# The output projection as a seven-product block form, product by product, with the up blocks laid out from it

## The chip, the cores and the metric

The kernel runs on one core of a Trainium2 chip. The metric is the time of one execution on the device in microseconds. Three runs of the kernel before took 1751.15, 1747.36 and 1748.91 us; the median is 1748.91 us. The core has five engines with queues of their own, which are worked off in order: TensorE (PE, matrix products into the accumulators in PSUM), VectorE (DVE), ScalarE (ACT), GpSimd (POOL) and SyncE (SP), which here issues the transfers between HBM and the on-chip memory. They wait for each other through semaphores.

## The reference

One layer of a hybrid decoder on 1032 tokens (1024 of a prompt, 8 single steps), width 1024:

```
proj = rmsnorm(x) @ w_in                  # split among two head groups
o_a  = HGRN2(q, k, v, f)                  # 8 heads of 128: 1024 columns
y    = SSD(xs, B, C, dt)                  # 16 heads of 64: 1024 columns
x    = x + concat([o_a, y]) @ w_out       # w_out: 2048 x 1024   <- the stage that changes
h    = rmsnorm(x, norm2_w)
gate, val = split(h @ w_up, 2)            # 2 x 2816 columns
x    = x + (silu(conv3(gate)) * val) @ w_down
y    = rmsnorm(x)
```

All data are 32-bit floats. Everything in the kernel is transposed: 128 features on the partitions, tokens along the free dimension.

## The kernel before

**Precision.** A product of 32-bit floats is made as three products of rounded parts: a weight tile is split into wh (rounded by ScalarE) and wl (the rest, by VectorE), rows into a high and a low part in the same way, and TensorE adds wh x high, wh x low and wl x high (`steps`, L305; all matmuls are recorded at L94).

**Stages.** The input projection runs as 52 jobs of 72 matmuls with 344 tokens each. The eight HGRN heads follow one another; the matmuls of a head are interleaved with the input projection of a later one (`drive`). Each head leaves its 128 rows in HBM (mix_d, eight head rows and eight state-space rows of 128 x 1032; L1055). Then comes the output projection, then the up projection, 22 jobs of 168 matmuls, then the down projection. Up and down already use a form with seven block products in place of eight (2 x 2 blocks of features in, features out and tokens): for the up projection it needs, for each instance of 516 tokens, seven blocks of rows p1 to p7, some of them sums and differences of normalised rows, each as a high and a low part. Down takes sums of weight blocks; these are made ahead, under the heads, by `down_sums`: load half a MB into the buffer wq (L193), four additions on GpSimd (L1202), store to wsum_d (L1204), load the next into the same buffer. There are 22 such items.

**The output projection before.** Jobs a, b, c, d: a is the state-space rows of the first 516 tokens, b the head rows of these tokens, c and d the same of the second 516. Each job multiplies 8 row tiles with one of 8 column tiles for two strips of 258 tokens, 48 matmuls; together 16 row tiles x 8 column tiles x 4 strips x 3 = 1536 matmuls of 258 tokens. The rows come back from mix_d (tile mx), are split on ScalarE (L1109) and VectorE (L1110); weights come as ws and are split at L1093 and L1094. ScalarE copies a's and c's result out of PSUM, VectorE adds b's and d's to it (L1168). The residual x is loaded token-major (xs, xd), turned by transposes on TensorE (four of 128 tokens and one small remainder for each of 16 items, L852 and L854) and added by VectorE (L847). Of each finished strip ScalarE squares the values, GpSimd sums the squares (n2r), and `set_norm` makes from them the inverse root on TensorE, ScalarE and VectorE (L698 to L701). `set_of(i)` then lays out instance i's seven blocks: normalisation on VectorE (L1320), the high part on ScalarE, the low part on VectorE (L1331, L1352), block sums on VectorE or GpSimd (L1336, L1348). Instance 0 is complete after job b, so that its blocks are laid out under c and d; instance 1's follow at the end of d and under the first up job.

**What sets the order.** TensorE's order is written out by hand: a step is one matmul, `after(n, ...)` and `spread(pieces, n)` place the other engines' work n steps later or every n steps. The scheduler orders the other engines from there. All transfers go through SP's queue in program order. A transfer into a buffer waits there until the buffer is free, and so does whatever stands behind it.

## Time and profile before

| what | value |
|---|---|
| median of three runs | 1748.91 us |
| the profiled execution | 1748.51 us, span 1746.6 us |
| busy: TensorE, VectorE, ScalarE, GpSimd | 98%, 68%, 48%, 28% of the span |
| first matmul of the output projection | at 831.25 us |
| first up job | begins at 1054.3 us |
| transfers | 239 MB, mean 137 GB/s |

The span runs from the first to the last recorded instruction; some 1.9 us of the execution lie around it. The page gives busy times over the whole span; a table by stretches, as quoted later, has in each row the stretch, its length, then for TensorE (PE), its weight loads (PEld), VectorE, ScalarE and GpSimd the busy time and number of instructions, then the granted clock (1.00 is full), the share of the DMA engines' time, and GB/s. A row of a group has its line, engine, operation, output and inputs, shapes, count, then busy time in us and the mean in ns, then idle time ahead of it and what ended it. A row of the timeline or the chain has the start, the duration and the count.

### The profile page before, as it was taken

The page shows a single profiled execution, that of the slowest core. Times are in us where ns is not written, and L with a number is a line of the kernel's source. Part 1 is how long each engine was busy: PE and PEld are TensorE (multiplying, and loading weights), DVE is VectorE, ACT ScalarE, POOL GpSimd, SP SyncE. Part 2 cuts the span into 40 slices and gives each one's busy share as a digit, 9 for nine tenths or more (in the row PEclk, how much of TensorE's full clock was granted, in tenths as well). Part 3 has the DMA queues.
Part 4 walks back from the last instruction along what each step waited for, and adds up shares of the span by engine and source line. Part 5 has one row for each costly group of instructions (what it writes and reads, how often), then busy time and mean ns, then how long its engine had stood idle before and what let it go on. Part 6 is the DMA issues. An engine that isn't in the chain of part 4 may idle for free.

```text
span 1746.6 us, 39082 instructions
## 1 busy us (share of the span) xinstructions
PE 1704.6 (98%) x15967; PEld 1650.3 (94%) x15967; DVE 1180.5 (68%) x2053; ACT 838.3 (48%) x1507; POOL 485.6 (28%) x500
## 2 busy tenths in 40 slices
PE   7999999999999999999999998999999999999998
PEld 7999998998999999999899998999999999999998
DVE  4657888467755655664755678867777777775664
ACT  6478688443443444444344444334433334444344
POOL 1102242111433422440102124554445554000001
PEclk9999999999999999999999999999999999999999
DMA  5133574563444443444556442323333323786463
GB/s 158 37 82 93 144 211 139 154 178 120 147 140 127 133 147 111 139 131 124 159 169 204 127 136 58 104 92 95 101 113 113 92 92 96 251 270 229 152 190 123
DMA packets 319689, 239.31 MB, mean 137 GB/s; under 512 B 18380, under 2 KB 287734, under 8 KB 319494
## 3 DMA queue, kind: packets, MB, share of 16 engines
q1 hardware_dynamic: 319222, 236.72, 45.1%
q8 instruction: 125, 2.05, 0.5%
q14 instruction: 54, 0.44, 0.1%
q0 software_dynamic: 288, 0.10, 0.0%
HBM read 178.18 MB, written 58.77 MB: 136 GB/s over the span
## 4 chain that ended last, share of the span: by engine, by line
PE 41%; DVE 4%; DMA 2%; ACT 1%; issue 1%; SPq 1%; DVEq 0%; ACTq 0%
PE ub L94 13%; PE dn L94 11%; PE ua L94 9%; PE mm L94 7%; DMA at<-act_d 1%; DMA ws<-in_w_out_dram 1%; DVE x L1320 1%; DVE wl L1094 0%; PE fin L1761 0%; SPq L193 0%; DVE ul L1331 0%; DMA x<-x_d 0%; DVE wl L1441 0%; DMA act_d<-fext 0%; DVE fcv L370 0%
## 5 line engine op out<-in xcount | busy, mean ns | idle before, releaser
L94 PE MATMUL mm<-hh,wh 128*128 128x344 f32 x1248 | 406.5, 326 | 0.0
L94 PE MATMUL mm<-hl,wh 128*128 128x344 f32 x1248 | 403.9, 324 | 0.0
L94 PE MATMUL mm<-hh,wl 128*128 128x344 f32 x1248 | 402.9, 323 | 0.0
L94 PEld LDWEIGHTS mm<-hh,wh 128*128 128x128 f32 x1248 | 234.9, 188 | 2.9 <-issue 0.9
L94 PEld LDWEIGHTS mm<-hh,wl 128*128 128x128 f32 x1248 | 235.1, 188 | 2.1 <-issue 1.0
L94 PEld LDWEIGHTS mm<-hl,wh 128*128 128x128 f32 x1248 | 234.9, 188 | 2.2 <-issue 0.9
L94 PE MATMUL ub<-uh,wh 128*128 128x258 f32 x704 | 199.4, 283 | 2.1 <-DVE fext L1491 1.6
L94 PE MATMUL ub<-ul,wh 128*128 128x258 f32 x704 | 199.6, 283 | 1.5 <-DVE ul L1352 1.5
L94 PE MATMUL ub<-uh,wl 128*128 128x258 f32 x704 | 198.8, 282 | 0.0
L94 PE MATMUL mm<-mx,wh 128*128 128x258 f32 x1024 | 190.9, 286 | 3.2 <-DVE mx L1110 2.3
L94 PEld LDWEIGHTS mm<-mx,wh 128*128 128x128 f32 x1024 | 158.5, 189 | 5.2 <-DVE mx L1110 2.7
L94 PE MATMUL dn<-at,wh 128*128 128x260 f32 (+1 forms) x896 | 163.1, 282 | 0.0
L94 PE MATMUL ua<-uh,wh 128*128 128x258 f32 x528 | 149.2, 283 | 1.1 <-ACT us L1463 0.6
L94 PE MATMUL ua<-ul,wh 128*128 128x258 f32 x528 | 148.9, 282 | 0.0
L94 PE MATMUL ua<-uh,wl 128*128 128x258 f32 x528 | 148.4, 281 | 0.0
L94 PE MATMUL mm<-mx,wl 128*128 128x258 f32 x512 | 145.4, 284 | 1.7 <-DVE wl L1094 1.7
L94 PEld LDWEIGHTS dn<-at,wh 128*128 128x128 f32 x896 | 137.6, 188 | 0.0
L1202 POOL TENSOR_TENSOR wq<-wq 128x256 f32<-128x256 f32 x88 | 83.3, 947 | 189.0 <-DMA wq<-in_w_down_dram 149.6
L94 PEld LDWEIGHTS ub<-uh,wh 128*128 128x128 f32 x704 | 132.9, 189 | 2.5 <-ACT uh L1330 1.8
L94 PEld LDWEIGHTS ub<-ul,wh 128*128 128x128 f32 x704 | 133.1, 189 | 1.9 <-DVE ul L1352 1.9
L94 PEld LDWEIGHTS ub<-uh,wl 128*128 128x128 f32 x704 | 133.1, 189 | 0.0
L94 PE MATMUL dn<-at,wl 128*128 128x260 f32 (+1 forms) x448 | 126.6, 283 | 2.8 <-DVE wl L1607 2.8
(341 smaller groups left out, 3711.9 us busy)
## 6 DMA issues: line engine op xcount, KB each, us to landing
ws<-in_w_in_dram SPq DMA_DIRECT2D x52, 512.0 KB
ws<-in_w_up_dram SPq DMA_DIRECT2D x44, 512.0 KB
at<-act_d SPq DMA_DIRECT2D x77, 258.0 KB
ws<-in_w_out_dram SPq DMA_DIRECT2D x36, 512.0 KB
wq<-in_w_down_dram SPq DMA_DIRECT2D x44, 256.0 KB
wsum_d<-wq SPq DMA_DIRECT2D x22, 512.0 KB
mx<-mix_d SPq DMA_DIRECT2D x32, 258.0 KB
csb<-cs_d SPq DMA_DIRECT2D x32, 256.0 KB
```

Of the source, the lines that this page charges most:

```text
L94: PE.matmul(out, lhsT, rhs, start=start, stop=stop)
L1202: G.tensor_tensor(out, x_, y_, op=ALU.add)
L1320: V.scalar_tensor_tensor(x_, x_, col("n2", m), rs, op0=ALU.mult, op1=ALU.mult)
```

## The change

The output projection becomes seven products as well. The 2048 rows are one block of state-space rows and one of head rows, the columns two halves (h = 0, 1), and the tokens are, for each instance i, the first and second 258 (c = 0, 1). The products run one after another, each over both instances: p1 (state-space rows, c = 0), p7 (state-space rows c = 0 less c = 1), p4, p6, p5, p2 (head rows, c = 0), p3. Each has 4 column tiles x 2 instances x 24 matmuls, so 7 x 192 = 1344 in all. p3 is cut into p3a (instance 0) and p3b (instance 1).

- The sums of weight blocks for p4 to p7 come from 16 new items ahead of the 22 for down, now 20 steps between an item's parts instead of 26 (`weight_sums`).
- The rows for p5, p6 and p3 are sums and differences of a head's rows and a state-space tile. Each head makes them when it is done (`row_sums`): it loads the state-space tile into its tile k, GpSimd makes three sums 516 wide, SP stores three half rows in row_d. The differences for p7 are made on VectorE when they are loaded.
- Results are combined out of PSUM as `out_add` says; the columns of c = 1 are complete after p5, those of c = 0 with h = 0 after p2, with h = 1 after p3.
- The residual is taken in 16 items of two feature tiles and 258 tokens, with four transposes and two small ones each, under p6, p5 and p2.
- The normalisation multiplies by the feature's weight on ScalarE and by the token's inverse root on VectorE. The blocks that need only c = 1 (p4, p5) are laid out under p2 and p3a (`second_halves`), the other five by `first_halves`, for instance 0 under p3b and for instance 1 in the first up job. This job takes p5 and p4 of both instances first, then the other five of instance 0, then those of instance 1.

```diff
+        fetch(k[:, :NT], mix_d[8 + h])
...
+        spread(row_sums(h, k, sg), 14)
+    def halves(t):
+        return t.rearrange("p (i c t) -> p i c t", i=2, c=2)
+    ROWS = ("p5", "p6", "p3")
+    MID = 2 * QW
+    row_d = dram.tile([3, 8, P, MID], F32, name="row_d")
+    def row_sums(h, k, sg):
+        a, b = halves(k[:, :NT]), halves(sg[:, :NT])
+        yield
+        yield
+        G.tensor_tensor(b[:, :, 1], a[:, :, 1], b[:, :, 1], op=ALU.subtract)
+        G.tensor_tensor(a[:, :, 0], b[:, :, 1], a[:, :, 0], op=ALU.subtract)
+        G.tensor_tensor(b[:, :, 0], a[:, :, 0], b[:, :, 0], op=ALU.add)
+        yield
+        for n, t in enumerate((b[:, :, 1], a[:, :, 0], b[:, :, 0])):
+            SP.dma_start(row_d[n, h].rearrange("p (i t) -> p i t", i=2), t)
...
+    def row_load(p, rs):
+        for r in rs:
+            hi, lo = (t.bitcast(F32).rearrange("p (i t) -> p i t", i=2) for t in (rows[p][r][:, :MID], rows[p][r][:, MID:]))
+            if p in ROWS:
+                fetch(lo, row_d[ROWS.index(p), r].rearrange("p (i t) -> p i t", i=2))
+            else:
+                fetch(lo, halves(mix_d[r if p in ("p2", "p4") else 8 + r])[:, :, 1 if p == "p4" else 0])
+            if p == "p7":
+                fetch(hi, halves(mix_d[8 + r])[:, :, 1])
...
+            if p == "p7":
+                d = tl("e", "dif")[:, :MID]
+                vbehind(lambda: V.tensor_tensor(d, x_, hi.bitcast(F32), op=ALU.subtract))
+                x_ = d
...
+    def out_add(p, i, m, ps):
+        x_ = lambda h, c: xf(i, h, c)[:, m]
+        if p == "p1":
+            mark[0] = A.copy(x_(0, 0), ps)
+        elif p == "p7":
+            mark[0] = A.copy(x_(1, 1), ps)
+        elif p == "p4":
+            vmark[0] = V.tensor_tensor(x_(0, 1), x_(1, 1), ps, op=ALU.add)
+        elif p == "p6":
+            vmark[0] = V.tensor_tensor(x_(1, 0), x_(0, 0), ps, op=ALU.add)
+            G.tensor_tensor(x_(0, 1), x_(0, 1), x_(1, 0), op=ALU.add)
+        elif p == "p5":
+            vmark[0] = V.tensor_tensor(x_(1, 0), ps, x_(1, 0), op=ALU.subtract)
+            G.tensor_tensor(x_(1, 1), x_(1, 0), x_(1, 1), op=ALU.subtract)
+            final(i, 0, 1, m)
+            final(i, 1, 1, m)
+        else:
+            h = int(p == "p3")
+            vmark[0] = V.tensor_tensor(x_(h, 0), x_(h, 0), ps, op=ALU.add)
+            final(i, h, 0, m)
...
+    def weight_sums():
+        yield from pair_sums(w_out[0].rearrange("(two i p) (gv h c) -> h i p two gv c", two=2, p=P, gv=2, h=2), wo_d, 1, 8)
+        yield from pair_sums(w_down[0].rearrange("(i two p) (gv h c) -> h i p two gv c", two=2, p=P, gv=2, h=2), wsum_d, 0, DK)
...
-    job("conv", None, once(lambda: (spread(conv_states(), 60), spread(down_sums(), 26))))
+    job("conv", None, once(lambda: (spread(conv_states(), 60), spread(weight_sums(), 20))))
...
-    for m in range(KT):
-        out_job(f"a{m}", 8, 0, m, begin={0: open_a, 2: ahead_b}.get(m))
-    for m in range(KT):
-        out_job(f"b{m}", 0, 0, m, begin={0: open_b}.get(m))
-    for m in range(KT):
-        out_job(f"c{m}", 8, 1, m, begin={0: open_c}.get(m), depth=3 if m < 7 else 4)
-    for m in range(KT):
-        out_job(f"d0{m}", 0, 1, m, (0,), {0: lambda: split_rest(0, 1)}.get(m), m > 3, "ttwwttww"[m], 2, 4)
-    for m in reversed(range(KT)):
-        out_job(f"d1{m}", 0, 1, m, (1,), pool="wwwwttww"[m], lead=2 if m > 1 else 1, depth=(2, 3, 3, 4, 4, 4, 5, 6)[m])
...
+    for p in OUT[:6]:
+        for m in range(4):
+            out_job(f"{p}_{m}", p, m, begin=begins.get((p, m)), depth=4 if (p, m) == ("p2", 3) else 3)
+    for m in range(4):
+        out_job(f"p3a{m}", "p3", m, (0,), {0: lambda: split_rest("p3")}.get(m), True, "ttww"[m], 2, 4)
+    for m in range(4):
+        out_job(f"p3b{m}", "p3", m, (1,), depth=4 - m if m else 4)
...
+    def normed(i, h, c):
+        x_ = xf(i, h, c)
+        r = rst(i, c).unsqueeze(1).to_broadcast([P, 2, QW])
+        for q in TWO:
+            for m in range(q.start, q.stop):
+                behind(lambda: A.activation(x_[:, m], x_[:, m], AF.Copy, scale=col("n2", 4 * h + m)))
+            vbehind(lambda: V.tensor_tensor(x_[:, q], x_[:, q], r, op=ALU.mult))
             yield
-        c0, c1 = slice(0, QW), slice(QW, MID)
-        if i == 0:
-            yield from norm(0)
-            yield from norm(1)
-            yield from put("p2", a2, "big")
-            yield from put("p4", b2, "e")
-        else:
-            yield from norm(1, c0)
-            yield from put("p2", a2, "big")
-            yield from norm(0, c0)
-            yield from put("p1", a1, "hT")
-            yield from norm(1, c1)
-            yield from put("p4", b2, "hT")
-            yield from norm(0, c1)
-        sa, sb = (quads(tl(tag, "sm")[:, :NT]) for tag in ("xe", "xc"))
-        if i:
-            yield from comb(sb, G, a1, b1, ALU.subtract)
-            yield from comb_put("p5", "hT", sa, b1, b2, ALU.subtract)
-            yield from comb_put("p6", "hT", sa, two(sa), a1, ALU.subtract)
-            yield from put("p7", [sb], "big")
-            yield from comb_put("p3", "big", sa, two(sa), a2, ALU.add)
-            return
-        yield from comb(sa, V, b1, b2, ALU.subtract)
-        yield from comb(sb, G, a1, b1, ALU.subtract)
-        while "c7" not in done:
+    def comb(t, x_, y_, op):
+        for q in TWO:
+            vbehind(lambda: V.tensor_tensor(t[:, q], x_[:, q], y_[:, q], op=op))
             yield
-        yield from put("p1", a1, "hT")
-        yield from put("p5", [sa], "hT")
-        yield from comb(sa, V, two(sa), a1, ALU.subtract)
-        yield from put("p6", [sa], "hT")
-        yield from put("p7", [sb], "hT")
-        yield from comb(sa, V, two(sa), a2, ALU.add)
-        yield from put("p3", [sa], "big")
+    def put(i, name, src, *tags):
+        hi, lo = (tl(tag, "u", F32R) for tag in tags)
+        hq, lq = quads(hi[:, :NT]), quads(lo[:, :NT])
+        usets[i][name] = hq, lq
+        for q in TWO:
+            setmark[0] = A.copy(hq[:, q], src[:, q])
+            vbehind(lambda: V.tensor_tensor(lq[:, q], src[:, q], hq[:, q].bitcast(F32), op=ALU.subtract))
+            yield
...
+    def second_halves(i):
+        b1, b2 = xf(i, 0, 1), xf(i, 1, 1)
+        yield from normed(i, 0, 1)
+        yield from normed(i, 1, 1)
+        sas[i] = quads(tl("xe", "sm")[:, :NT])
+        yield from comb(sas[i], b1, b2, ALU.subtract)
+        yield from put(i, "p4", b2, "big", "e" if i else "big")
+        while i and "p2_3" not in done:
+            yield
+        yield from put(i, "p5", sas[i], *(("hT", "hT") if i else ("e", "big")))
+    def first_halves(i):
+        a1, a2, b1, sa = xf(i, 0, 0), xf(i, 1, 0), xf(i, 0, 1), sas[i]
+        yield from normed(i, 0, 0)
+        yield from put(i, "p1", a1, "hT", "hT")
+        yield from comb(sa, sa, a1, ALU.subtract)
+        yield from comb(b1, a1, b1, ALU.subtract)
+        yield from put(i, "p6", sa, "hT", "hT")
+        yield from put(i, "p7", b1, "hT", "big")
+        yield from normed(i, 1, 0)
+        yield from comb(sa, sa, a2, ALU.add)
+        yield from put(i, "p2", a2, "hT", "big")
+        yield from put(i, "p3", sa, "hT", "big")
...
-    FIRST = ("p1", "p2", "p4", "p5", "p6", "p7", "p3")
+    FIRST = ("p5", "p4", "p1", "p6", "p7", "p2", "p3")
...
-        after(36, lambda: spread(set_of(0), 14))
...
+        after(20, lambda: set_norm(0, 1))
+        after(34, lambda: set_norm(1, 1))
+        sets = chain(second_halves(0), second_halves(1))
+        after(40, lambda: spread(sets, 9))
+        finish("p2_3")
...
+        finish("p3a3")
+        after(28, lambda: set_norm(0, 0))
+        sets0 = first_halves(0)
+        after(32, lambda: spread(sets0, 3))
+        for m in range(3):
+            finish(f"p3b{m}")
+            after(3, lambda m=m: up_split(0, m))
+        finish("p3b3")
+        for _ in chain(sets, sets0):
...
-        after(24, lambda: spread(second, 1))
-        for _ in ups(0, [(name, i) for i in range(2) for name in FIRST]):
+        after(24, lambda: spread(first_halves(1), 3))
+        for _ in ups(0, [(name, i) for names in (FIRST[:2], FIRST[2:]) for i in range(2) for name in names]):
```

What moves on VectorE, where the output projection runs into the up projection. Before, these rows stand ahead of the eviction of product p6 for the first instance in the first up job (us, the last row; x1 are the output columns, n2r the inverse root, uh and ul the parts of a block, sm a block sum):

```order
L701 SCALAR_TENSOR_TENSOR n2r_125_798<-nt_1502_12513,n2r_125_798 128x258
L1320 SCALAR_TENSOR_TENSOR x1_1375_11574<-x1_1375_11574,vcol_99,n2r_125_798 128x258 x2
L1320 SCALAR_TENSOR_TENSOR x1_1394_11727<-x1_1394_11727,vcol_99,n2r_125_798 128x258 x2
L1331 TENSOR_TENSOR ul_1507_12539<-x1_1375_11574,uh_1506_12538 128x516
L1320 SCALAR_TENSOR_TENSOR x1_1327_11246<-x1_1327_11246,vcol_99,n2r_125_798 128x258
L1331 TENSOR_TENSOR ul_1507_12539<-x1_1394_11727,uh_1506_12538 128x516
L1320 SCALAR_TENSOR_TENSOR x1_1327_11246<-x1_1327_11246,vcol_99,n2r_125_798 128x258
L1320 SCALAR_TENSOR_TENSOR x1_1350_11406<-x1_1350_11406,vcol_99,n2r_125_798 128x258 x2
L1348 TENSOR_TENSOR sm_1508_12554<-x1_1327_11246,x1_1375_11574 128x516
L1348 TENSOR_TENSOR sm_1508_12554<-x1_1350_11406,x1_1394_11727 128x516
L1467 TENSOR_TENSOR us_1523_12618<-us_1499_12498,ub_1522_12605 128x258
```

Now these are the last rows ahead of the same eviction (u are the parts of a block); 28 more rows of the same kinds stand ahead of them, behind the addition of p3b's first product:

```order
L1370 TENSOR_TENSOR x1_1134_9737<-x1_1134_9737,n2r_1357_11510 128x516 x2
L1375 TENSOR_TENSOR sm_1459_12208<-sm_1459_12208,x1_1134_9737 128x516
L1384 TENSOR_TENSOR u_1523_12656<-x1_1134_9737,u_1522_12655 128x516 x2
L1375 TENSOR_TENSOR sm_1459_12208<-sm_1459_12208,x1_1134_9737 128x516
L1375 TENSOR_TENSOR x1_1262_10862<-x1_1134_9737,x1_1262_10862 128x516 x2
L1384 TENSOR_TENSOR u_1529_12691<-sm_1459_12208,u_1528_12690 128x516 x2
L1384 TENSOR_TENSOR u_1532_12704<-x1_1262_10862,u_1531_12703 128x516 x2
L1370 TENSOR_TENSOR x1_1305_11176<-x1_1305_11176,n2r_1357_11510 128x516 x2
L1375 TENSOR_TENSOR sm_1459_12208<-sm_1459_12208,x1_1305_11176 128x516 x2
L1384 TENSOR_TENSOR u_1536_12739<-x1_1305_11176,u_1535_12738 128x516
L1489 TENSOR_TENSOR us_1537_12742<-us_1533_12718,ub_1534_12720 128x258
```

All that is left of both instances' blocks but for three low parts now stands in front of this eviction; before, instance 0's blocks were long done there and most of instance 1's sums and low parts stood behind it.

What moves on SP's queue, between the last head and the third product. Before, the rows of the next part and its weights follow each other (ws are weights, mx rows, x1_d the stores of finished columns):

```order
L193 DMA mx_1257_10672<-mix_d_123 128x516
L193 DMA mx_1258_10674<-mix_d_123 128x516
L1179 DMA x1_d_797<-x1_1139_9673 128x258
L1081 DMA ws_1263_10738<-in_w_out_dram 128x8x128
L1179 DMA x1_d_797<-x1_1139_9673 128x258
L1401 DMA ws_1370_11564<-in_w_up_dram 128x8x128
L1401 DMA ws_1371_11566<-in_w_up_dram 128x8x128
L1179 DMA x1_d_797<-x1_1139_9673 128x258
L1081 DMA ws_1270_10804<-in_w_out_dram 128x8x128
```

Now, at the corresponding place, loads and stores of the weight sums (wq, wsum_d) stand between the row loads and the next product's weights:

```order
L193 DMA mx_1248_10783<-row_d_797 128x516
L193 DMA wq_1243_10705<-in_w_down_dram 128x2x256 x2
L193 DMA mx_1249_10784<-row_d_797 128x516
L193 DMA mx_1250_10785<-row_d_797 128x516
L193 DMA mx_1251_10786<-row_d_797 128x516
L193 DMA mx_1252_10787<-row_d_797 128x516
L1264 DMA wsum_d_800<-wq_1243_10705 128x8x128
L193 DMA mx_1253_10788<-row_d_797 128x516
L193 DMA mx_1254_10789<-row_d_797 128x516
L193 DMA mx_1255_10790<-row_d_797 128x516
L193 DMA wq_1259_10819<-in_w_down_dram 128x2x256 x2
L1125 DMA ws_1263_10864<-wo_d_799 128x1024
```

Each of these items still waits for its buffer and for GpSimd, and the weight ws that closes the piece, of p4's last column tile, now stands behind two of them.

At the end of a head (here the last), its store of rows (mix_d) is now followed by the row sums:

```order
L1075 DMA mix_d_123<-sg_1104_9566 128x1032
L193 DMA wq_1235_10611<-in_w_down_dram 128x2x256 x2
L1125 DMA ws_1241_10698<-wo_d_799 128x1024
L193 DMA mx_1207_10402<-mix_d_123 128x2x258
L1094 DMA row_d_797<-sg_1104_9566 256x1x258
L1094 DMA row_d_797<-k_1068_9169 256x1x258
L1094 DMA row_d_797<-sg_1104_9566 256x1x258
L1264 DMA wsum_d_800<-wq_1235_10611 128x8x128
```

The three stores to row_d and the load of the state-space tile are new in each head; before, the head's store was the last of it.

360 lines of the change are left out of this document (162 added, 198 removed).

## The prediction

> **What bounds the kernel now.** I read the page first (busy shares, the slices, the costliest groups), then the same busy times by stretches of the output projection, then the chain of waits inside it.
>
> ```profile
> span 1746.6 us, 39082 instructions
> PE 1704.6 (98%) x15967; PEld 1650.3 (94%) x15967; DVE 1180.5 (68%) x2053; ACT 838.3 (48%) x1507; POOL 485.6 (28%) x500
> L94 PE MATMUL mm<-mx,wh 128*128 128x258 f32 x1024 | 190.9, 286 | 3.2 <-DVE mx L1110 2.3
> L94 PE MATMUL mm<-mx,wl 128*128 128x258 f32 x512 | 145.4, 284 | 1.7 <-DVE wl L1094 1.7
> ```
>
> TensorE is busy for 98% of the span, so removed matmuls come off the end, unless another engine then holds TensorE up. The output projection is the two mm<-mx groups: 1024 + 512 = 1536 matmuls. Their mean of 286 ns is not their price, because they overlap; the chain gives the price:
>
> ```profile
> 957.59 5.96 PE mm L94 x48
> 963.55 0.44 PE xtp L852 x4
> 963.98 0.15 PE xtd L854
> 964.14 5.98 PE mm L94 x48
> ```
>
> 48 matmuls take 5.97 us, 0.1244 us each. The four residual transposes of an item take 0.44 us (0.11 each) and the small one 0.15.
>
> ```profile
> core 0: us, PE busy (x) PEld busy (x) DVE busy (x) ACT busy (x) POOL busy (x), PEclk, DMA share, GB/s
> 900.00:950.00 50.00, 50.00 (x417) 49.81 (x416) 23.43 (x36) 18.75 (x33) 9.06 (x13) 1.00 0.67 200
> 1000.00:1020.00 20.00, 18.77 (x153) 18.16 (x151) 15.49 (x20) 11.17 (x16) 4.05 (x3) 1.00 0.49 132
> 1020.00:1040.00 20.00, 19.76 (x161) 19.50 (x162) 12.63 (x23) 8.75 (x16) 6.84 (x6) 1.00 0.42 119
> 1040.00:1060.00 20.00, 18.86 (x153) 18.34 (x152) 14.96 (x24) 9.53 (x17) 8.24 (x9) 1.00 0.50 146
> 1060.00:1080.00 20.00, 16.38 (x131) 15.61 (x130) 19.96 (x32) 8.88 (x17) 8.08 (x8) 1.00 0.00 1
> 1080.00:1100.00 20.00, 19.37 (x162) 19.16 (x161) 17.43 (x28) 9.56 (x17) 11.17 (x9) 1.00 0.27 81
> ```
>
> In the middle of the output projection (900 to 950) TensorE never stops and VectorE is half idle. Where it runs into the up projection (1000 to 1100), TensorE is idle for 1.23 + 0.24 + 1.14 + 3.62 + 0.63 = 6.9 us, and from 1060 to 1080 VectorE is busy for 19.96 of 20 us: there, for a moment, VectorE is the bound, laying out the second set of up blocks.
>
> **The matmuls.** Seven products of 192 matmuls make 1344, against 1536. 192 x 0.1244 = **-23.9 us**; the pace of the up projection, which I expect as the other bound, is a little faster per matmul, 5.79 / 48 = 0.1206:
>
> ```profile
> 1083.27 5.79 PE ub L94 x48
> ```
>
> That would make it 23.2 us. The residual is still 16 items, each now with four transposes and two small ones: one more of 0.15 each, **+2.4 us** on TensorE's own queue, which nothing hides.
>
> **The layout of the up blocks.** This is the large term. Before, the first token half is finished in the middle of the stage and its seven blocks are laid out while TensorE runs on and VectorE is half idle. Now both instances finish last, and the blocks that need the last product's columns are all laid out between that product and the first up job. VectorE works in order, so I count its rows. From the addition after p3b's first product to the eviction of p6 for the first instance (us_1537; the second instance's p6 needs its accumulator) stand 8 normalisations, 12 block sums and 19 low-part differences 516 wide, 7 weight differences 512 wide, 5 additions 258 wide and two inverse roots of three operations. Rows that price them:
>
> ```profile
> L1094 DVE TENSOR_TENSOR wl<-ws,wh 128x1024 fp32r<-128x1024 f32 x35 | 45.1, 1288 | 18.2 <-ACT wh L1093 17.5
> L1168 DVE TENSOR_TENSOR x<-x,mm 128x258 f32<-128x258 f32 x32 | 13.4, 418 | 13.1 <-PE mm L94 13.1
> L1331 DVE TENSOR_TENSOR ul<-x,uh 128x516 fp32r<-128x516 f32 x12 | 8.2, 712 | 1.9 <-ACT uh L1330 1.8
> L1441 DVE TENSOR_TENSOR wl<-wt,wh 128x512 fp32r<-128x512 f32 x8 | 5.7, 738 | 0.2 <-ACT wh L1440 0.2
> ...
> 1058.06 0.42 DVE L699 SCALAR_TENSOR_TENSOR nt<-n2ms,n2r 128x258 f32<-128x258 f32 x1
> 1058.51 0.85 DVE L700 SCALAR_TENSOR_TENSOR nt<-nt,n2r 128x258 f32<-128x258 f32 x1
> 1059.40 1.39 DVE L701 SCALAR_TENSOR_TENSOR n2r<-nt,n2r 128x258 f32<-128x258 f32 x1
> ...
> 1067.01 2.21 DVE L1348 TENSOR_TENSOR sm<-x,x 128x516 f32<-128x516 f32 x2
> 1069.14 0.41 DVE L1467 TENSOR_TENSOR us<-us,ub 128x258 f32<-128x258 f32 x1
> 1069.48 1.29 DVE L1352 TENSOR_TENSOR ul<-sm,uh 128x516 fp32r<-128x516 f32 x2
> 1070.69 1.29 DVE L1348 TENSOR_TENSOR sm<-sm,x 128x516 f32<-128x516 f32 x2
> 1071.90 0.41 DVE L1475 TENSOR_TENSOR us<-us,ua 128x258 f32<-128x258 f32 x1
> ```
>
> In an unbroken run two 516-wide operations take 1.21 us from start to start (1069.48, 1070.69, 1071.90), so 0.605 each: the floor. The group means (0.71, 0.74) are the ceiling, and the pair at 1067.01, with an operation of GpSimd beside it, took 2.21. Floor: 46 x 0.605 + 5 x 0.34 (1069.14 to 1069.48) + 2 x 2.77 (1058.06 to 1060.83) = 27.8 + 1.7 + 5.5 = 35.0 us. Ceiling: 39 x 0.71 + 7 x 0.74 + 5 x 0.42 + 5.5 = 40.5. Count from the end of p3a: the first of these rows can start when the first p3b product is done, 24 x 0.1244 = 3 us on, and I add 1 us for two places where VectorE waits for ScalarE's root. So the eviction is done 39 to 44.5 us after p3a. Behind it TensorE still has the second instance's p6, p7, p2 and p3 of that up job, 48 matmuls or 5.8 us, with two evictions between, some 7 us: the job ends 46 to 51.5 us after p3a. Without a wait it would be 96 matmuls of p3b and the job's 168: 11.9 + 20.3 = 32.2 us. TensorE loses 14 to 19 us. I take the lower half, **+16 us**, since most rows are the streaming kind. The 6.9 us of today's wait at the same place are inside this count, so they come off: **-6.9 us**.
>
> One stage earlier, under p2 and p3a, 58 VectorE instructions (wl, the halves for the second columns, the row differences, the residual) sum at the floor to 6 x 1.29 + 26 x 0.605 + 13 x 0.34 + 4 x (0.605 + 0.15) + 5.5 = 36 us, against 11 groups of 24 matmuls and four residual items on TensorE: 264 x 0.1244 + 4 x 0.74 = 35.8. That is 0 to 4 us over, and the three accumulators let TensorE lead by as much: I take **+1 us**, keeping 5 as its upper end. Under p6 and p5 it is about 20 us of VectorE for 24 us of TensorE: nothing.
>
> **The queue that issues transfers.** SP issues in order. Rows of the trace for the weight sums that already exist:
>
> ```profile
> 589.04 1.04 POOL L905 TENSOR_TENSOR vb<-vb,k 128x512 f32<-128x512 f32 x1 [6.70 <-DMA vb<-vd_d]
> 594.55 5.17 POOL L1202 TENSOR_TENSOR wq<-wq 128x256 f32<-128x256 f32 x4
> 607.40 3.50 POOL L1202 TENSOR_TENSOR wq<-wq 128x256 f32<-128x256 f32 x4 [7.69 <-DMA wq<-in_w_down_dram]
> ...
> 582.37 0.34 SPq L1055 DMA_DIRECT2D mix_d<-sg  x1
> ...
> 599.74 0.37 SPq L1204 DMA_DIRECT2D wsum_d<-wq  x1
> 603.15 1.20 SPq L193 DMA_DIRECT2D wq<-in_w_down_dram  x2
> 610.92 0.36 SPq L1204 DMA_DIRECT2D wsum_d<-wq  x1
> 613.06 0.38 SPq L200 DMA_DIRECT2D ws<-in_w_in_dram  x1
> 614.13 1.21 SPq L193 DMA_DIRECT2D wq<-in_w_down_dram  x2
> ...
> 644.45 0.34 SPq L1055 DMA_DIRECT2D mix_d<-sg  x1
> ...
> 626.21 1.05 ACT L203 CAST wh<-ws 128x1024 fp32r<-128x1024 f32 x1 [2.59 <-PE mm L94]
> ```
>
> One item (load, four GpSimd sums, store, all in one buffer) takes 614.13 - 603.15 = 11 us: landing 4.25, sums 3.5, store and return 3.2. There are now 38 items instead of 22, 60 steps of the order apart instead of 78. Per head of 288 steps that is 4.8 items: 52.8 us, about 7 more where the head's own GpSimd work stands ahead (589.04 to 594.55, and a slower sum of 5.17), about 4 for the three new row sums, that is 64 us in a head of 62 (from 582.37 to 644.45, when the rows of one head and of the next leave). The lag of about 2 us per head piles up to 10 to 13 over six and a half heads. A weight that is issued at 613.06 is cast at 626.21; with 4.25 us of landing, 8.9 us of lag cost nothing before the cast, and more is hidden behind it, as the next job's weights are cast while the last ones are in use. I take **0**, 0 to 8 from the rows, and the other end is a rival.
>
> From head 7's end to p6 the queue carries, one behind another, seven weights, four sum loads and three stores of half a MB, the head's rows, three row stores and nine row loads: 11.0 MB, and p4's last weight stands behind two sum items of 11 to 12 us each. By the issue times this weight is 0 to 10 us late; **+3 us**, nearer the low end as the weight before it is already there.
>
> ```profile
> GB/s 158 37 82 93 144 211 139 154 178 120 147 140 127 133 147 111 139 131 124 159 169 204 127 136 58 104 92 95 101 113 113 92 92 96 251 270 229 152 190 123
> ```
>
> The volume alone, 11.0 MB in the 36 us that TensorE needs until then (288 matmuls at 0.1244), asks for 306 GB/s, where the best slice has 270; at 270 it takes 41 us, 5 us more, which one job's lead (48 matmuls, 6 us) just hides. The Trainium skill (DMA: Bandwidth & Descriptors, Specifications) puts the limit of HBM per core at about 358 GB/s; by that the 11.0 MB fit in 31 us and this bound falls away. No slice of the row above comes near it, so the row keeps its place as the upper side.
>
> The clock is a second place. The column PEclk stands at 1.00 in every stretch above, but none of them holds a long wait. The Trainium skill (TensorE: Matmul & The Clock Gate, HAM oscillation) says that an idle gap over about 3.4 us sends TensorE back to half clock for a while; if the new wait comes as two or three such gaps, its figure of 1.67 us at half pace makes an estimate of about 2 us more on top of the sum. The rows above neither show nor exclude it.
>
> **The sum.** -23.9 + 2.4 + 16 - 6.9 + 1 + 0 + 3 = **-8.4 us**. Against the profiled execution's 1748.5 us (span 1746.6 and 1.9 around it; the median of the three runs, 1748.9, is 0.4 above) that is **1740 us**. Its own bounds: 14 for the layout and 0 for the queue give 1734, 19 with 1 + 4 and 6 give 1750.
>
> **The rivals.**
> *A, the saving arrives whole*: the layout hides as well as today, -23.9 + 2.4 = 1727 us. For it: VectorE has 32% of the span idle. Against it: that idle time lies in other stages, and in the place that counts VectorE is already full from 1060 to 1080 with fewer operations.
> *B, the layout eats it all*: the ceiling prices, with GpSimd's sums beside them as at 1067.01, make the wait 19 us plus 4 under p2, the queue 6: 1749 us, no change.
> *C, slower*: the chain of weight sums. If an item takes 11.6 us rather than 11 (the sums took 3.5 in one row and 5.17 in the other), a head needs 4.8 x 11.6 + 11 = 66.7 us against 62.1; from the point where the lag passes the 8.9 us of cover, TensorE goes at the queue's pace: 4.6 x 6.5 - 8.9 = 21 us, 1761 us. For it: one buffer, in order, and the new row stores behind the same queue. Against it: in the trace SP often waits beside these items without TensorE noticing.
> *D, the change doesn't shorten what it should*: the matmuls fall but take longer each (their rows are now two strips of 258); then the sum lacks its 23.9 us, 1764. Against it: each matmul still reads one strip of 258.
>
> **Chances.** The forecast 0.43, A 0.14, B 0.12, C 0.28, D 0.03. A difference under 0.2% (3.5 us) is what a measurement of this kernel can't tell from none. The forecast's own range, 1734 to 1750, lies mostly beyond that: 0.38 faster, 0.04 within, 0.01 slower. With A that is 0.52 faster; B gives 0.09 within and 0.03 on the faster side; C and D 0.31 slower. So faster 0.55, the same 0.13, slower 0.32. The range reaches from just under A to D, a little over C's price: 1726 to 1764.
>
> **What will show it.** Right: 1344 mm matmuls at 0.124 us each; TensorE whole from p7 to p5 but for about 3 us in p4; at the change to the up projection one stretch of 40 us or so in which VectorE is full and TensorE loses 14 to 19 us, waiting for the evictions us and the blocks ul. Wrong: TensorE waits for new weights during the heads, and these for SP's turn (C); waits of less than 8 us at the transition (A); or waits inside p4 and p6 for weights above 10 us. The forecast falls if the heads no longer take about 62 us each, as I have given that nothing.

## The result, and the profile after

The changed kernel takes 1873.03 us (median of six runs, 1863.98 to 1875.5) against 1749.65 us for the kernel before (six runs): 1.0698 of its time, 95% interval 1.0675 to 1.0722. The forecast was 1740 us, with a range up to 1764. One execution of the kernel before, beside the last runs, took 2051.3 us at a granted clock of 0.753 and is left out of all comparisons. The page of the changed kernel:

```profile
span 1873.7 us, 39110 instructions
PE 1725.9 (92%) x15791; PEld 1664.7 (89%) x15791; DVE 1222.5 (65%) x2086; ACT 849.6 (45%) x1544; POOL 595.2 (32%) x600
L94 PE MATMUL mm<-mx,wh 128*128 128x258 f32 x896 | 179.1, 298 | 14.2 <-ACT wh L1136 7.7
```

896 and 448 matmuls (the second group is not shown) are the 1344 that were expected. TensorE is idle for 147.8 us of the span, before for 42.0. And it is busy for 21.3 us longer, although 21.5 us of work by the forecast's prices were taken out: the mean matmul of this group takes 298 ns, not 286. Where the stages begin is seen from the first and last start of three groups, here before (after the colon least, median and longest duration in ns, then the starts in us; ua and ub are the two accumulators of the up projection, which begins with ua before the change and with ub after it):

```profile
L94 PE MATMUL mm<-mx,wh x1024: 276/283/471, 831.2 to 1053.9; 128*128 128x258 f32 x171
L94 PE MATMUL ua<-uh,wh x528: 277/282/385, 1054.1 to 1503.9; 128*128 128x258 f32 x176
L94 PE MATMUL dn<-at,wh x896: 275/282/368, 1504.2 to 1735.7; 128*128 128x260 f32 x90, 128*128 128x256 f32 x90
```

and after:

```profile
L94 PE MATMUL mm<-mx,wh x896: 276/283/583, 904.6 to 1168.3; 128*128 128x258 f32 x180
L94 PE MATMUL ub<-u,wh x1408: 276/283/419, 1168.5 to 1626.8; 128*128 128x258 f32 x176
L94 PE MATMUL dn<-at,wh x896: 274/282/420, 1629.9 to 1861.5; 128*128 128x260 f32 x90, 128*128 128x256 f32 x90
```

| stage | before, us | after, us | difference | of this TensorE busy | clock after |
|---|---|---|---|---|---|
| up to the first product of the output projection | 831.2 | 904.6 | +73.4 | +16.9 | 0.94 from 428 us on |
| from there to the first up matmul | 222.9 | 263.9 | +41.0 | -0.3 | 0.90 |
| to the first down matmul | 450.1 | 461.4 | +11.3 | +3.6 | 0.99 |
| to the end of the span | 242.4 | 243.8 | +1.4 | +1.1 | 0.98 |

The last column is the mean granted clock of the changed kernel; before, it is 0.99 or 1.00 in each of these stages. More than half of the loss lies ahead of the stage that was rewritten, in the heads. Before, a head took 62 us in the mean, from one store of its rows to the next; after, it takes 73.8. Here are the second and the third of these stores after the change, 76.9 us apart (before 64.4):

```profile
540.40 0.34 SPq L1075 DMA_DIRECT2D mix_d<-sg  x1
...
545.81 0.57 SPq L1094 DMA_DIRECT2D row_d<-sg  x1
547.31 0.57 SPq L1094 DMA_DIRECT2D row_d<-k  x1
549.03 0.51 SPq L1094 DMA_DIRECT2D row_d<-sg  x1
552.72 3.52 SPq L927 DMA_DIRECT2D out_dram<-Sh  x2
...
558.12 1.25 SPq L193 DMA_DIRECT2D wq<-in_w_out_dram  x2
566.32 0.39 SPq L1264 DMA_DIRECT2D wo_d<-wq  x1
566.81 0.53 SPq L200 DMA_DIRECT2D ws<-in_w_in_dram  x1
...
580.74 1.20 SPq L193 DMA_DIRECT2D wq<-in_w_out_dram  x2
581.99 1.15 SPq L193 DMA_DIRECT2D Sh<-in_state_hgrn_dram  x2
...
617.34 0.34 SPq L1075 DMA_DIRECT2D mix_d<-sg  x1
```

This is SP's queue. From 540.4 to 558.1 it gets out the row sums and the states, which GpSimd has to finish first; only then comes the next weight sum. Behind three loads of weight sums stands Sh, the load of the next head's decode states, which leaves at 581.99. The timeline of VectorE and of TensorE at that place:

```profile
586.31 0.69 DVE L925 TENSOR_TENSOR Sh<-Sh,f 128x512 f32<-128x512 f32 x1 [14.62 <-POOL wq L1262]
...
587.19 0.59 PE L94 MATMUL odp<-selod,odr 128*128 128x8 f32 x2 [9.79 <-DVE fbufT L357]
```

VectorE stood for 14.6 us in front of the scaling of these states. The profile names GpSimd's sum of weights as the releaser, but this sum doesn't touch Sh, and the load of Sh was issued 4.3 us earlier, about the time that a load of the same size takes to land in the prediction's rows (4.25 us): most likely it is the load that was missing. A small copy (fbufT), which empties an accumulator, stands behind the scaling in VectorE's queue, and TensorE waits 9.8 us for it. This was not the only head. VectorE's idle time ahead of the twelve scalings of six heads, before:

```profile
  POOL wq L1202: 9.5, 3
  DMA Sh<-in_state_hgrn_dram: 5.1, 2
  DMA rt<-in_state_conv_ffn_dram: 4.4, 1
```

and after:

```profile
  POOL wq L1262: 65.1, 5
  DMA Sh<-in_state_hgrn_dram: 13.7, 1
```

That is 78.8 us in place of 19.0. The summary of TensorE's waits over the whole run (total us, times, longest):

```profile
PE a L94 <- DVE q L944: 29.7, 11, 7.1
PE o L94 <- DVE SS L1030: 27.7, 4, 9.5
PE xtp L851 <- DMA xs<-in_x_prompt_dram: 19.9, 3, 10.7
PE n2ms L94 <- POOL n2r L1249: 10.0, 1, 10.0
PE odp L94 <- DVE fbufT L357: 9.8, 1, 9.8
PE mm L94 <- ACT wh L1136: 7.7, 2, 4.7
```

Lines one, two and five are the heads. xtp is the residual's transposes, wh the weights of p4, n2ms the layout at the end. The rest is for the most part the clock; four stretches around the longest wait (the third figure from the right is the granted clock):

```profile
1030.00:1036.00 6.00, 0.00 (x0) 0.00 (x0) 0.00 (x0) 3.50 (x6) 0.00 (x0) 0.50 1.06 337
1038.00:1040.00 2.00, 2.00 (x10) 2.00 (x10) 1.08 (x3) 0.00 (x0) 0.46 (x1) 0.50 0.66 173
1042.00:1044.00 2.00, 2.00 (x12) 1.47 (x11) 0.35 (x1) 0.00 (x0) 0.00 (x0) 0.73 0.22 80
1044.00:1046.00 2.00, 2.00 (x19) 2.00 (x18) 1.56 (x5) 1.05 (x1) 0.65 (x1) 1.00 0.33 96
```

TensorE comes back at 1036.4 and works at half clock up to about 1043: 10 to 12 matmuls in 2 us, then 19. The Trainium skill (TensorE: Matmul & The Clock Gate, HAM oscillation) says that an idle gap over some 3.4 us brings this; the trace agrees for this wait of 10.7 us, which cost about 3 us more behind it.

### The profile page after: what moved, and what is told of

It is laid out like the page before. It is cut to its first block, busy times and chain, and to the rows that moved or that the text cites. A ratio compares the mean times of both kernels' runs of the same rounds, so it can differ in the third digit from the quotient of the medians.

```text
span 1873.7 us, 39110 instructions
## 1 busy us (share of the span) xinstructions
PE 1725.9 (92%) x15791; PEld 1664.7 (89%) x15791; DVE 1222.5 (65%) x2086; ACT 849.6 (45%) x1544; POOL 595.2 (32%) x600
## 5 line engine op out<-in xcount | busy, mean ns | idle before, releaser
L94 PE MATMUL ub<-u,wh 128*128 128x258 f32 x1408 | 257.8, 284 | 1.4 <-DVE us L1489 1.4
L1262 POOL TENSOR_TENSOR wq<-wq 128x256 f32<-128x256 f32 x152 | 135.8, 894 | 352.1 <-DMA wq<-in_w_down_dram 178.6
L94 PEld LDWEIGHTS ub<-u,wh 128*128 128x128 f32 x1408 | 219.5, 191 | 1.8 <-DVE us L1489 1.7
L94 PE MATMUL ub<-u,wl 128*128 128x258 f32 x704 | 200.2, 284 | 0.0
L94 PE MATMUL ua<-u,wh 128*128 128x258 f32 x1056 | 193.5, 284 | 1.0 <-DVE us L1497 0.5
L94 PEld LDWEIGHTS ua<-u,wh 128*128 128x128 f32 x1056 | 163.7, 189 | 1.4 <-DVE val L1520 0.7
L94 PE MATMUL ua<-u,wl 128*128 128x258 f32 x528 | 149.5, 283 | 0.0
L94 PEld LDWEIGHTS ub<-u,wl 128*128 128x128 f32 x704 | 134.1, 190 | 0.1
L1463 DVE TENSOR_TENSOR wl<-wt,wh 128x512 fp32r<-128x512 f32 x88 | 81.2, 941 | 50.7 <-ACT wh L1462 50.2
L94 PEld LDWEIGHTS ua<-u,wl 128*128 128x128 f32 x528 | 100.0, 189 | 0.0
```

The costliest lines, as they stand in the source:

```text
L94: PE.matmul(out, lhsT, rhs, start=start, stop=stop)
L1262: G.tensor_tensor(out, x_, y_, op=ALU.add)
L1463: V.tensor_tensor(lo[:, cs], sums[name], hi[:, cs].bitcast(F32), op=ALU.subtract)
```

## The experiments

Single runs unless an interval stands with them; the kernel before took 1742 to 1754 us beside them. "Start" is the first product of the output projection (831.2 before, 904.6 after), "out" the time from there to the first up matmul (222.9, 263.9), "up" from there to the first down matmul (450.1, 461.4), all in us. Three runs that leave the heads of the change as they are start at 904.6, 901.7 and 902.7: some 3 us are scatter.

| run | total | start | out | up |
|---|---|---|---|---|
| no row sums | 1835.65 | 868.2 | 262.7 | 460.4 |
| slow pace of the weight sums | 1824.76 | 855.2 | 240.4 | 485.3 |
| both | 1798.15 | 828.9 | 236.4 | 488.6 |
| GpSimd issues the stores | 1859.85 | 891.7 | 263.2 | 461.5 |
| residual loads early | 1855.06 | 901.7 | 248.5 | 461.6 |
| both of these | 1835.97 | 885.9 | 244.2 | 461.5 |
| before, 20 steps | 1781.82 | 862.0 | 224.3 | 450.7 |
| residual early, root late | 1857.12 | 902.7 | 248.7 | 461.1 |
| operands free | 1749.00 | 828.3 | 216.7 | 460.6 |
| slow pace, first row sum out of place | 1821.40 | 851.7 | 241.4 | 485.1 |
| the same, row stores by GpSimd (A) | 1817.37 | 848.1 | 240.4 | 486.0 |
| all repairs | 1801.85 | 846.6 | 220.8 | 490.0 |
| A without GpSimd's row sums | 1810.07 | 839.7 | 238.6 | 487.2 |
| A without the load of the tile | 1824.94 | 853.8 | 241.2 | 487.3 |
| before, 30 steps | 1749.38 | 829.1 | 225.4 | 451.8 |

**Row sums and weight sums, apart and together.**

```diff
-        spread(row_sums(h, k, sg), 14)                   # first and third run
-        fetch(k[:, :NT], mix_d[8 + h])
...
-    ... spread(weight_sums(), 20)                        # second and third run
+    ... spread(islice(wsums, 72), 26)                    # 24 items under the heads
+        spread(wsums, 70)                                # 14 items from up job 1 on
```

> The changed kernel without the row sums: no load of the state-space tile, no three GpSimd sums and no three stores per head; the third kind of rows is read as it lies in HBM, so p5, p6 and p3 are computed from other rows. A head took about 75 us (540.4 to 617.3 between two head stores), 62 before. Theory S (the weight sums, an item every 60 steps, hold SP's queue): heads stay above 70 us, total 1855 to 1870. Theory R (the row sums push everything at the head's turn back by some 13 us): heads fall to 62 to 64 us, total about 1790.

> The changed kernel with all row sums, but the weight sums at the pace of before under the heads (26 steps between an item's parts, 24 items), and the other 14 items under up jobs 1 to 19, so that none is left in the output projection. Theory S: heads fall to 62 to 65 us, and the output projection (264 us from its first matmul to the first up matmul, of which some 40 lie in p7 to p6) loses 15 to 30 us of waits; total about 1775. Theory R: heads stay above 70 us; total 1840.

> Both: slow pace, 14 items under the up jobs, and no row sums (p5, p6, p3 from other rows). By either theory the heads are back at 62 us and start the output projection near 832 us. What is then left above 1748.5 - 21.5 = 1727 us belongs to the output projection and its end: 16 us by the prediction's count, so about 1743; more if the loads of the residual and the row loads are late without the weight sums as well.

Without row sums the output projection starts 36.4 us earlier, with the slow pace 49.4, with both 75.7, the whole loss of the heads. So each theory holds for a part: alone, the two parts would add up to 85.8 us, and some 10 us of them are the same (the row sums are 26.3 where the pace is slow). The idle time of VectorE ahead of the scalings of Sh goes down too, from 78.8 us to 53.1 without row sums and to 23.1 at the slow pace; with both it is 22.2. What the row sums still cost at the slow pace is therefore not in this wait.

The slow pace also takes 23.5 us off the output projection, where items no longer stand in SP's queue, and puts 24 us on the up projection, which was not expected: there VectorE waits 16.5 us in 13 places for GpSimd's part of the evictions (1.2 us in 2 places in the change), as GpSimd now has the sums to do as well. The third run was expected at about 1743 us and took 1798.15; of the 55 us, 27 are in the up projection (488.6) and the most of the rest in the output projection (236.4).

**The pace in the kernel before.**

```diff
-    ... spread(down_sums(), 26)
+    ... spread(down_sums(), 20)                          # or 30
```

> The kernel before, with one number changed: its 22 weight sums 20 steps apart instead of 26. Nothing else of the change is in it. Theory S (an item that comes every 60 steps, 13 us, in one buffer, is too fast for the queue): the heads in which the sums still run get 5 to 9 us longer, 69 to 71 instead of 62.3, until the 22 items are out some 300 us after 428; the total rises by 25 to 40 us, as 49 us in the changed kernel were for six and a half heads. If the pace harms only beside the row sums, the heads stay at 62 us and the total within 5 us of before.

> The kernel before with its 22 weight sums 30 steps apart instead of 26: the other side of the run with 20 steps, which cost 31 us in the heads. If the loss starts only below some pace between 60 and 78 steps an item, nothing changes (within 2 us). If it goes on with the pace, the heads gain the 3 to 4 us that TensorE still idles in them, 1745 us.

One number of the kernel before costs 30.8 us in its heads, where the change lost 73.4. VectorE's idle time ahead of the scalings of Sh is 44.4 us in this run, 19.0 in the kernel before. With 20 steps two of its head stores, in which the sums still run, are

```profile
532.82 0.35 SPq L1055 DMA_DIRECT2D mix_d<-sg  x1
...
603.94 0.34 SPq L1055 DMA_DIRECT2D mix_d<-sg  x1
```

71.1 us apart, where the last heads, without sums, take 62 and 64. With 30 steps next to nothing is gained: the ratio to before is 0.9988 (0.9977 to 0.9999), and the start moves by 2 us. So the loss sets in between 60 and 78 steps an item; where, no run shows.

**Who waits on the queue.**

```diff
-                SP.dma_start(dst[h]..., t...)            # weight sums
+                G.dma_start(dst[h]..., t...)
-            SP.dma_start(row_d[n, h]..., t)
+            G.dma_start(row_d[n, h]..., t)
```

> The changed kernel with nothing left out; only the stores of the weight sums and the three row stores of each head are issued by GpSimd, right behind its own sums, and no longer by SP. The first runs gave 49 us of the heads' 73 to the weight sums and 26 to 36 to the row sums. Theory W (the harm is SP, standing in order before a store that waits for GpSimd, with the heads' weights and states behind it; that wait is 102 us for the weight sums' stores and some 25 for the row stores between 450 and 905 us): heads fall from 75 us to 62 to 66, first product of the output projection at 835 to 850 instead of 904.6, total about 1810. Theory V (the harm is the volume moved or GpSimd's own time): heads stay above 70 us, total above 1850.

The start moves by 12.9 us, not by 55 to 70: theory W fails. The numbers are those of theory V (72.6 us a head, 1859.85 in all), but this run does not show that its causes, the volume or GpSimd's time, are the right ones. In the summary of SP's waits under the heads (450 to 905 us) the wait for GpSimd's weight sums, 102.0 us in the change, is gone, and another has grown from 56.9 us to 130.7:

```profile
SPq L193 <- DMA wo_d<-wq: 71.3, 11, 9.9
SPq L193 <- DMA wsum_d<-wq: 59.4, 9, 9.3
```

SP now stands in front of the next load, until the store has emptied the one buffer. The queue is still held by the round of this buffer, whoever issues the store. VectorE's idle time ahead of Sh falls to 35.5 us, but TensorE's wait for a behind q rises from 29.7 to 46.0: most of the loss has only moved.

**The residual's loads.** They stand in SP's queue behind eight row loads. The first load of each of three batches left it at 1031.6, 1072.0 and 1109.5 us; TensorE stood in front of them from 1025.6, 1073.1 and 1109.9 us on. So the expectation's 2 to 4 us between load and use did not exist in any of the three.

```diff
-        after(2, lambda: spread(late, 20))               # late2, late3 in the same way
+        next(late)                                       # loads, 24 to 96 matmuls ahead
+        after(22, lambda: spread(late, 20))
```

> The changed kernel with nothing left out; only the loads of the residual are issued 24 to 96 matmuls earlier, ahead of the eight row loads of the next product, and their first transposes 20 to 36 matmuls later. If the 19.9 us in which TensorE waits for these loads (10.7, 3.6, 5.6) come from standing behind the row loads with 2 to 4 us between load and use, they fall to under 3 us and the output projection from 264 us to about 245; the heads do not change. If DMA bandwidth is what makes them late, TensorE waits as long at the same places or for the rows that now stand behind.

> Both of the above. Theory W and the order of the residual's loads together: 75 - 64 = 11 us for each of six and a half heads and about 20 in the output projection, total about 1785. What then stays above 1727 is the weight sums inside the output projection (24 us by the run with the slow pace) and the layout at its end (13 us).

15.4 us come off the output projection, and of 19.9 us of waits 6.0 stay, where under 3 were expected. For the most part it was the order of the queue. The longest wait was partly the weight sums': the store of one of them left at 1027.2 us, ahead of these loads, and in the run with the slow pace, with no such item there, the three waits are 15.3 us. The two changes together take 18.7 us off the heads and 19.7 off the output projection; their gains alone add up to 15.8 and 16.1. The total of 1785 us did not come, as the heads had not fallen as theory W said.

**The layout at the end.**

```diff
-        after(20, lambda: set_norm(1, 0))
-        after(24, lambda: spread(first_halves(1), 3))
+        after(72, lambda: set_norm(1, 0))
+        after(76, lambda: spread(first_halves(1), 2))
```

> The kernel with the earlier residual loads, and one step more: the inverse root of the last strip is asked of TensorE 72 matmuls into the first up job, not 20, and the second instance's blocks follow it 4 steps later, 2 apart. In all runs so far TensorE stood 10 us at this small product, waiting for GpSimd's sum of squares. Theory D (VectorE's chain of some 38 us sets the end, as predicted): the wait moves to the evictions us or the blocks u, and the first up job ends within 3 us of the same place; the time from the first up matmul to the first down matmul stays at 461 us. Theory N (TensorE stands in order before a product that is not ready, with ready ones behind): this time falls by 7 to 10 us.

Theory D: "up" is 461.1 us against 461.6 in the run with the early residual, on which this one is built. TensorE no longer waits 10 us at the small product; it waits 4.3 us for an eviction and 2.4, 1.3 and 1.1 for blocks instead. That VectorE's chain sets the end of this piece is seen in the changed kernel itself, in the row from the addition of p3b's first product (1159.5) to the eviction us_1537 (at 1197.24):

```profile
1159.50:1197.60 38.10, 26.76 (x196) 25.98 (x194) 36.36 (x58) 25.84 (x56) 17.22 (x11) 0.87 0.05 15
```

VectorE is busy for 36.4 of these 38.1 us.

**What is left of the row sums.**

```diff
-        G.tensor_tensor(b[:, :, 1], a[:, :, 1], b[:, :, 1], op=ALU.subtract)
+        G.tensor_tensor(a[:, :, 1], a[:, :, 1], b[:, :, 1], op=ALU.subtract)
```

> The kernel with the slow pace (24 items under the heads, 14 under the up jobs), and the first row sum put into the tile that was just loaded, not over the head's own rows, so that GpSimd need not wait until these have been stored (4.1 us before the sum at 544.5). In the slow-pace run the heads end at 855.2, without row sums at 828.9. If that wait is the harm of the row sums, the heads end near 835; if it is the three stores and the load that stand in SP's queue, they end within 5 us of 855.

> The run with the first row sum out of place (heads end at 851.7), and the three row stores of a head issued by GpSimd behind its sums instead of SP. If SP's standing in front of these stores is what is left of the row sums' harm (829 without them), the heads end at 832 to 840; if it is the load of the tile, GpSimd's 4 to 5 us of sums or the stores' volume, they stay at 848 to 855.

> The run with GpSimd's row stores (heads end at 848.1; without all row work at 828.9), less GpSimd's three sums per head; load and three stores stay, so the rows stored are not sums. If GpSimd's 4.5 us ahead of the next head's states is what is left of the harm, the heads end at 829 to 834. If the transfers are, at 844 to 850.

> The same run, with the three sums and stores but without the load of the state-space tile (the sums take what stands in the tile). If this load, which stands in SP's queue behind the last use of the tile with the next weights behind it, is what is left, the heads end at 829 to 836; if not, at 844 to 850. If sums and load both give a part, both runs end between.

Of 26.3 us the wait for the head's own store is 3.5, SP's wait for GpSimd's sums 3.6 (both hardly above the scatter), and the sums themselves 8.4. The load is none of it: without it the start is 5.7 us later, which I can't explain. Some 11 us stay, with the load and the three stores together, and are open. The last two runs ended outside all that was expected of them (839.7 and 853.8). How three GpSimd sums cost TensorE anything is seen in a group of VectorE's small operations at the head's start, with the sums

```profile
L946 DVE TENSOR_TENSOR tt<-f 128x512 f32<-128x512 f32 x6 | 10.9, 1818 | 0.0
```

and without them:

```profile
L946 DVE TENSOR_TENSOR tt<-f 128x512 f32<-128x512 f32 x6 | 4.9, 809 | 0.0
```

Its seven operations of a head (L946) take 5.7 us with the sums beside them (34.0 in six heads) and 2.3 without (14.0). TensorE's wait for the chain that they belong to, the products a behind q, is 21.3 us with the sums and 12.1 without. Over the whole of 450 to 850 us VectorE is busy for 250.3 us with them and 239.4 without; single groups of the chain are shorter with them (q<-q,tt 31.1 us, without 35.5), so these rows show the cost and not its full account. The Trainium skill (GPSIMD Engine Reference, Specifications) has GpSimd and VectorE share their path to the on-chip memory when VectorE reads two inputs from it; the two rows agree.

**What the seven products are worth, and the best version.**

```diff
-            return wo_d[m // 2, SUMS.index(p), m % 2]    # operands free
+            return w_out[0, :8 * P, m * P:(m + 1) * P]...
```

> What the seven products are worth if their operands cost nothing: the changed kernel without row sums and without the 16 weight sums of the output projection (p4 to p7 use plain weight blocks, p5, p6 and p3 other rows, so that these products have other inputs of the same size), the 22 weight sums for down at the pace of before, and the residual's loads early. Heads as before (first product near 831). Theory F (the prediction's own count for the end of the stage, 13 to 16 us at the layout, nothing else): 1727 + 13 = 1740, 5 to 8 us under before. Theory G (the output projection has still more waits of its own, for split rows, roots and reduced clock; 236 us with the loads late, 15 of them the residual): first product to first up matmul 220, not 203; total 1755 to 1760, above before even with free operands.

> All repairs found so far in one kernel that leaves nothing out: slow pace of the weight sums (24 items under the heads), the other 14 under the up jobs with each of their four additions on its own step, row sums out of place with GpSimd's stores, residual loads early. From the single runs: heads end at 832 to 850, output projection 222 to 226, first up to first down matmul 465 instead of 482, 244 behind it: 1765 to 1785. It beats the changed kernel by 5%, and does not reach the kernel before, as the layout and the waits inside the output projection take back what the 192 matmuls save.

With free operands the kernel takes 1749.0 us (span 1746.9, before 1746.6): no faster. The heads are whole (828.3), and the output projection is 6.2 us shorter, where 21.5 us of work by the forecast's prices are missing:

```profile
L94 PE MATMUL mm<-mx,wh x896: 276/283/582, 828.3 to 1044.8; 128*128 128x258 f32 x180
L94 PE MATMUL ub<-u,wh x1408: 276/283/419, 1045.0 to 1502.5; 128*128 128x258 f32 x176
L94 PE MATMUL dn<-at,wh x896: 274/282/368, 1505.6 to 1735.8; 128*128 128x260 f32 x90, 128*128 128x256 f32 x90
```

"Up" is 460.6, 10.5 more than before, the layout. Of the 15.3 us that are missing in the output projection 9.6 are more idle time of TensorE and 5.8 more busy time, at a granted clock of 0.98. The largest wait inside the output projection, 7.5 us, is at p7's rows:

```profile
849.68 0.70 DVE L1148 TENSOR_TENSOR dif<-mx 128x516 f32<-128x516 f32 x1 [7.89 <-DMA mx<-mix_d]
```

The difference of two row tiles stands in VectorE's queue 7.9 us before the first of p7's sixteen loads has landed (they begin to leave at 845.8), and head 7's operations k and q stand behind it.

The kernel with all repairs takes 1801.85 us, 1.0303 of before (1.0286 to 1.0320): 71 us better than the change, and still slower than before. It was expected at 1765 to 1785. Putting each addition of an item on its own step did not help the up projection (490 us, not 465). The rest of its loss is the row sums (start 846.6), the 14 items under the up jobs and the layout. No run here points to a version of the seven products that beats the kernel before.

## Why the prediction was wrong

**Right: the work removed.** There are 1344 matmuls, and where the clock is whole each takes 0.120 us (45 of them start in the 5.42 us from 1146.84 to 1152.26). At this pace the work taken out, less the added transposes, is 20.7 us, near the forecast's 21.5.

**Right: the layout.** The forecast was 14 to 19 us in place of 6.9. "Up" is 11.3 us longer (10.5 with free operands), and the waits that it had before come to 4.7 us: 15 to 16 us. The eviction us_1537 is done at 1197.65 us, 41 us after the addition of p3a's last product begins (1156.61); the count of VectorE's rows gave 39 to 44.5. Only the place of the wait was another: TensorE stood at the small product for the root, ahead of this eviction.

**Right in size: p2 and p3a.** The forecast was 1, at most 5 us; the waits for VectorE and ScalarE there are 1.8 (the root), 0.2, 1.8 and 1.0 us, 4.8 in all, so the upper end.

**Wrong: "I take 0, 0 to 8 from the rows" for the queue under the heads.** It was 73.4 us, and the heads took 73.8 us each, which the prediction had named as the sign of its fall. The cause was rival C's, SP's queue, priced at 21 us; the path was not, as no wait for a weight is among TensorE's waits in the heads. Three things in its sum failed. The cover of 8.9 us was read from a weight, between its load and its cast; the load that came too late first was that of the decode states Sh, which stands behind three loads of weight sums and has VectorE's in-order queue behind it. The load of these states was in the order and in the trace of before; its cover had not been counted. VectorE's idle time there rose by 59.8 us. Second, the row sums were priced as 4 us of GpSimd a head; 26 to 36 us in all came of them. The sums beside VectorE's chain are 8.4 of these us, the waits for a store and in SP's queue some 7, and about 11 are not settled. Third, the item of 11 us was nearly right (11.7 and 11.0 between loads at 558.1, 569.8 and 580.7), and the count of 64 us for a head of 62 let the lag grow by 2 us a head. The run of before with 20 steps, which has no row sums, took 71 to 72 us for each of three heads: 60 steps are too few with the head's own transfers alone, and by more than the count of GpSimd's and SP's rows shows.

**Wrong: "+3 us" for the queue up to p6.** The weight sums inside the output projection cost 23.5 us (the change against the run with the slow pace), the clock included. The waits for wh and wl, between 997 and 1016 us, are 4.7, 1.1, 3.0 and 0.8 us: not the last weight of p4 alone was late, as the prediction had it, but the one before it too. The direction was right, the size not.

**Missing: the residual's loads.** The sum priced their extra transposes (2.4 us) and not the loads, which left SP's queue, behind eight row loads, only when TensorE stood in front of them or was about to: 15.4 us. Missing too: p7's differences in VectorE's queue ahead of head 7's work, a wait of 4.0 us in the changed kernel and of 7.5 with free operands.

**Wrong by more than ten: the clock.** The estimate was 2 us for two or three gaps. TensorE's busy time is 21.3 us up where it should be 21.5 down. These 43 us or so are put down to a slower clock after many gaps: 21 in the output projection (granted clock 0.90), 17 in the heads (0.94), 4 in the up projection. The kernel before with 20 steps supports this: with the same matmuls as before TensorE is busy for 12.8 us longer, at 0.989.

The parts for the output projection: 23.5 for the weight sums, 4.0 for the row sums (240.4 to 236.4), 15.4 for the residual and 15.3 that stay with free operands (216.7 against 222.9 - 21.5) are 58.2 of the 62.5 us that were lost there. They come from different runs and are not quite apart, as the residual's longest wait shows; the rest is not told apart. Of the forecast's rivals, A fell with free operands: even then the saving does not arrive.

## What to carry to other kernels

Before work is put into an in-order queue, follow every transfer that stands behind it to the engine that waits, and take the cover of the one that is late first; the weights' cover said nothing of the states'. A background chain in one buffer has a pace at which it is free (here an item every 78 steps) and one, not far from it (60), at which all that shares the queue pays: it can be found by changing that one number in the kernel as it is. And a wait of several us on TensorE costs more than itself: here the matmuls behind a wait of 10.7 us ran at half clock for 6.6 us.

## What was not expected of the hardware

The half clock went on long after TensorE was back: for 6.6 us where it had idled 10.7 us (1036.4 to 1043.0) and for 5.3 us where it had idled 9.8 us (587.2 to 592.5), against the 1.67 us that the estimate took from the Trainium skill (TensorE: Matmul & The Clock Gate, HAM oscillation). The page's figure is of a kernel that works for only about 2 us between its waits, so it was no measure for an engine that goes on working. And shorter waits sufficed: behind one of 3.0 us, with one of 0.8 us right after it, the granted clock was 0.50 from 1016 to 1019 us.

The prediction's 270 GB/s was no upper bound. It was read off slices of 43.7 us; over 10 us the kernel before already moved 334 GB/s (950 to 960 us), and a stretch under p7's loads in the changed kernel moved 358:

```profile
930.00:940.00 10.00, 7.21 (x173) 6.76 (x174) 9.25 (x15) 4.42 (x8) 0.00 (x0) 1.00 1.09 358
```

The Trainium skill's limit of about 358 GB/s per core (DMA: Bandwidth & Descriptors, Specifications) was the better figure. In the run with the slow pace 10 us moved 363 GB/s (880 to 890); no run shows whether this is a limit. And a VectorE operation of 512 elements took 1818 ns in place of 809 in the mean, with three more GpSimd sums per head.
